# Beginning every second weight transfer of the experts' part on GpSimd instead of SyncE

## The chip, the cores and the metric

The kernel runs on one core of one Trainium2 chip. The metric is the device time of one launch in microseconds (us). TensorE (PE), VectorE (DVE), ScalarE (ACT), GpSimd (POOL) and SyncE (SP) each have an instruction stream of their own; 16 DMA engines move data between the chip's memory (DRAM here) and the on-chip buffers. Any engine's stream can begin a transfer; the transfer then runs by itself and tells of its landing through a semaphore.

## The reference

One decoder block over 256 tokens of width 1024: a modulated norm, one large input projection, a convolution branch and a gated recurrence branch that are merged and added to x, and then a mixture of 32 experts in which each token uses its top 4. Only the experts' part is touched by the change:

```python
logits = hf @ w_router + b_router
top_val, top_idx = lax.top_k(logits, 4)
top_w = softmax(top_val)
# for every token and each of its four experts e:
u = xb @ w1[e] + b1[e]                  # w1[e] is 1024 x 2048, float32
y = clamped_swiglu(u) @ w2[e] + b2[e]   # w2[e] is 1024 x 1024, float32
out[token] += top_w * y
```

All 32 experts are computed, so all of w1 and w2 is read: 32 times 12 MiB.

## The kernel before

The kernel has a first part (modulation, projection, the two branches, merge, router) and then the experts' part. All weights pass through one pool of 22 buffers (`NSLOT`) of 8 KB per partition. `queue` (L117) writes down what is to be loaded, in the order of use; `load` (L120) takes the next entry, takes a buffer and begins the transfer on SyncE (L123); `pump` (L126) decides how many loads are made whenever `free` returns a buffer. In the first part `pump` follows a plan, `LOADS`, whose entries add up to 88 loads. 73 entries stand in the queue ahead of the experts' weights, so the plan also makes the first 15 of the experts' loads. From L1207 on `spare` is a number: every freed buffer is used for the next load at once.

An expert takes 12 transfers of 1 MiB: 8 of w1 (`first_layer`, L972 to L999, matmuls on L987) and 4 of w2 (`second_layer`, matmuls on L1026). The last expert's w2 comes in 5 pieces with shorter rows, and one transfer of 512 KB (`gfin`) stands before the last expert.

Expert 0 to 31 follow one another in a Python loop, fully unrolled. From expert 3 on the loop is `inline`: after the first layer a branch (`tc.If`, L1247) looks whether the expert has more than 64 tokens and then treats a further 32 of them, and a second branch (L1278) does the second layer for these. The buffers of w1 are given back, all eight at once, only behind the first branch, those of w2 behind the second. Every engine executes these branches, each in its own stream.

After expert 21 (`RELOAD_AFTER`) stands `reload` (L1123), for tokens that fit nowhere else. It takes three buffers of the pool (`ring`, L1140), and its body, a loop over experts that loads weights with transfers begun on GpSimd, stands inside a branch at L1143. On the data here the body is not executed; each engine jumps over it. Behind the jump GpSimd's stream has a few semaphore instructions and one that brings the semaphores of its transfers to the counts which they would have if the body had run. The three buffers are given back right after (`free(3)`), and the next three loads of weights use them. x2, the residual stream, keeps one of the 22 buffers through the whole of the part.

In the experts' part the order of instructions is written out by hand for TensorE and SyncE (`manual_schedule`); GpSimd is not in that list, and it has no transfers and no arithmetic there. On SyncE a load waits for two things: for its buffer to be free, and for one of eight semaphores, which the loads take in turn, to be free again: the load eight places earlier must have landed.

Of the kernel before, what the change touches and what calls it, by code (L numbers as in the profile page):

```python
# [90 lines left out]
def block_kernel(ctx, tc, xT_d, x_d, prm_d, con_d, wada0_d, wada_d, bada_d, gfin_d, win_d, wco_d, who_d, wo_d,  # L91
                 wr_d, br_d, w1_d, b12_d, w2_d, out_d):
    nc = tc.nc
# [10 lines left out]
    loaded = {}  # L104
    plan = iter(LOADS)
    spare = None

    def slot(shape, name, dt=F32):
        live[0] += 1
        assert live[0] <= NSLOT, name  # L110
        return big.tile(shape, dt, tag="s", name=name)
# [8 lines left out]
    def load():  # L120
        key, shape, src, into = pending.pop(0)
        t = into if into is not None else slot(shape, "w_" + "_".join(map(str, key)), src.dtype)
        nc.sync.dma_start(out=t, in_=src)  # L123
        loaded[key] = t

    def pump():  # L126

        if spare is None:
            for _ in range(next(plan, 0)):
                load()  # L130
        else:
            while pending and live[0] < NSLOT - spare:
                load()

    def fetch(key):
        while key not in loaded:
            load()
        return loaded.pop(key)
# [1068 lines left out]
    spare = 0  # L1207
# [4 lines left out]
    for e in range(E_RUN):  # L1212
        i = e % 2
        hot = hot_of(e)
        spare = 3 if e == RELOAD_AFTER else 0
# [66 lines left out]
        if e == RELOAD_AFTER:  # L1282
            reload()
            spare = 0
# [132 lines left out]
```

## Time and profile before

| | us |
|---|---|
| median of 3 runs | 1334.53 |
| lowest and highest | 1331.17, 1335.19 |
| the profiled execution, as a run | 1334.8 |
| its span, first to last instruction | 1333.1 |
| busy: TensorE matmul | 1225.6 (92%) |
| busy: VectorE, ScalarE, GpSimd | 547.8, 274.2, 145.4 |
| bytes moved | 480.57 MB |

The span is the time from the first to the last instruction of one profiled execution; 1.7 us of that run lie around it. A busy TensorE is not a TensorE at its peak, and shares over the whole span mix the first part, in which GpSimd does arithmetic and the DMA engines have pauses, with the experts' part, in which GpSimd is idle and the DMA engines are not. The profile is therefore read by stretches.

### The profile page before, as it was taken

The numbers are of one execution on the slowest core, as the hardware profiler recorded it, in microseconds if no ns is written. First come the engines' busy times: TensorE is split into PE (matmuls) and PEld (weight loads), VectorE is DVE, ScalarE is ACT, GpSimd is POOL, SyncE is SP. The second block draws the span as 40 slices with busy tenths as digits, with TensorE's granted clock in tenths as the row PEclk, the third lists the DMA queues.
The fourth block names the chain that finished last, engine by engine and source line by source line (L and its number), as shares of the span: only waits on it lengthen the run. The fifth ranks groups of instructions, "written<-read, shape, count | busy, mean of one in ns | idle before, by whom it ended". The sixth has DMA issues, their size and how long they took to land. (4 is left out here: it accounts for less than half of the span.)

```text
span 1333.1 us, 18930 instructions
## 1 busy us (share of the span) xinstructions
PE 1225.6 (92%) x7761; PEld 671.4 (50%) x7761; DVE 547.8 (41%) x1065; ACT 274.2 (21%) x434; POOL 145.4 (11%) x63
## 2 busy tenths in 40 slices
PE   5999999999899999999899898888898889999997
PEld 3899877679864343443434333232333324334432
DVE  4498999645844242333223313222223312323322
ACT  4445534653321010101001000000000000000112
POOL 3257535122300000000000000000000000000000
PEclk8999989999999999999999999999899998999999
DMA  9993435646689999999999999999999999989994
GB/s 380 412 394 112 145 128 221 235 174 235 251 314 405 420 420 419 420 420 420 421 419 420 420 420 420 420 421 420 420 420 418 419 421 420 418 347 420 419 419 168
DMA packets 71493, 480.57 MB, mean 360 GB/s; under 512 B 7488, under 2 KB 8768, under 8 KB 16064
## 3 DMA queue, kind: packets, MB, share of 16 engines
q1 hardware_dynamic: 70928, 477.99, 88.0%
q8 instruction: 94, 1.54, 0.5%
q10 hardware_dynamic: 432, 0.72, 0.2%
q14 instruction: 39, 0.32, 0.1%
HBM read 477.63 MB, written 1.05 MB: 359 GB/s over the span
## 5 line engine op out<-in xcount | busy, mean ns | idle before, releaser
L987 PE MATMUL u_gl<-w_w,xg 128*64 128x512 f32 x1024 | 273.5, 599 | 23.5 <-DMA w_w<-in_w_dram 23.4
L987 PE MATMUL u_lin<-w_w,xg 128*64 128x512 f32 x1024 | 272.1, 594 | 0.8 <-issue 0.8
L1026 PE MATMUL yp<-w_w,li 128*64 128x512 f32 x992 | 223.3, 602 | 13.5 <-ACT li L1013 10.2
L994 DVE TENSOR_SCALAR gl<-u_gl 128x512 f32<-128x512 f32 (+1 forms) x33 | 22.3, 675 | 338.9 <-PE u_gl L987 338.9
L987 PEld LDWEIGHTS u_gl<-w_w,xg 128*64 128x64 f32 x1024 | 77.1, 137 | 166.7 <-issue 92.0
L987 PEld LDWEIGHTS u_lin<-w_w,xg 128*64 128x64 f32 x1024 | 81.9, 137 | 139.5 <-issue 139.5
L386 PEld LDWEIGHTS p_ps<-h,ws 128*128 128x128 f32 x1152 | 141.2, 193 | 11.7 <-issue 5.9
L386 PE MATMUL p_ps<-h,ws 128*128 128x256 f32 x1152 | 146.2, 287 | 0.0
L1026 PEld LDWEIGHTS yp<-w_w,li 128*64 128x64 f32 x992 | 69.1, 138 | 149.8 <-issue 128.0
L1036 DVE TENSOR_TENSOR yg<-yp,ga 64x512 f32<-64x512 f32 x60 | 41.3, 689 | 233.0 <-PE yp L1026 232.4
L372 POOL TENSOR_TENSOR ws<-w_in,ws 128x1024 fp32r<-128x1024 f32 x45 | 114.0, 2549 | 121.9 <-ACT ws L370 113.6
L995 ACT ACTIVATE u_gl<-gl 128x512 f32<-128x512 f32 (+1 forms) x33 | 19.4, 589 | 407.8 <-DVE gl L994 407.7
L437 DVE SCALAR_TENSOR_TENSOR cv<-u,pre,cv 128x255 f32<-128x255 f32 (+25 forms) x240 | 95.1, 456 | 9.1 <-ACT cv L434 8.3
L951 PE MATMUL xg_ps<-o,w_x 128*128 128x128 f32 (+1 forms) x544 | 68.6, 286 | 17.4 <-DVE li L996 10.3
L951 PEld LDWEIGHTS xg_ps<-o,w_x 128*128 128x128 f32 x544 | 65.0, 199 | 30.6 <-DVE li L996 21.7
L370 ACT CAST ws<-w_in 128x1024 fp32r<-128x1024 f32 x64 | 65.9, 1046 | 47.9 <-PE p_ps L386 25.0
L1039 ACT ACTIVATE ys0h<-yg,by 64x512 fp32r<-64x512 f32 x30 | 21.6, 720 | 244.0 <-DVE yg L1036 244.0
L955 DVE TENSOR_SCALAR xg<-xg_ps,g,sh 128x128 f32<-128x128 f32 (+1 forms) x136 | 45.4, 395 | 25.0 <-issue 16.6
L1013 ACT COPY li<-ta 128x512 f32<-128x512 f32 (+1 forms) x33 | 18.9, 573 | 120.6 <-PE ta L1010 120.6
L372 DVE TENSOR_TENSOR ws<-w_in,ws 128x1024 fp32r<-128x1024 f32 x19 | 25.0, 1331 | 14.0 <-ACT ws L370 14.0
L386 PE MATMUL wo_ps<-ws,mg 128*128 128x256 f32 x192 | 26.2, 297 | 3.5 <-ACT ws L370 1.8
L1040 DVE SCALAR_TENSOR_TENSOR ys0l<-yg,by,ys0h 64x512 fp32r<-64x512 f32 x30 | 22.4, 748 | 12.8 <-ACT ys0h L1039 11.9
(286 smaller groups left out, 1111.3 us busy)
## 6 DMA issues: line engine op xcount, KB each, us to landing
w_w<-in_w_dram SPq DMA_DIRECT2D x383, 1024.0 KB, 19.9
w_in<-in_win_dram SPq DMA_DIRECT2D x32, 1024.0 KB, 12.2
w_ada<-in_wada_dram SPq DMA_DIRECT2D x24, 1024.0 KB, 16.1
w_ho<-in_who_dram SPq DMA_DIRECT2D x4, 1024.0 KB, 4.7
w_co<-in_wco_dram SPq DMA_DIRECT2D x4, 1024.0 KB, 5.1
w_wo<-in_wo_dram SPq DMA_DIRECT2D x4, 1024.0 KB, 8.3
xT<-in_xT_dram SPq DMA_DIRECT2D x1, 1024.0 KB, 7.2
w_x<-in_x_dram SPq DMA_DIRECT2D x1, 1024.0 KB, 6.5
```

The source lines that it names most:

```text
L370: nc.scalar.copy(out=to[:, 0], in_=w[:, ks, :])
L372: (nc.vector if dve else nc.gpsimd).tensor_tensor(out=to[:, 1], in0=w[:, ks, :], in1=to[:, 0].bitcast(F32), op=ALU.subtract)
L386: nc.tensor.matmul(out, lhsT=lt, rhs=rh, start=first and kt == 0 and i == 0, stop=kt == KT - 1 and i == 2, skip_group_check=not first)
L437: nc.vector.scalar_tensor_tensor(out=cv[:, ct, s:], in0=u[i][:, m, :T - s], scalar=tap, in1=cv[:, ct, s:], op0=ALU.mult, op1=ALU.add)
L951: nc.tensor.matmul(ps[:, i, cs], lhsT=x2[:, t, kt * P:(kt + 1) * P], rhs=o[:, 0, t, cs], start=t == 0, stop=t == NT - 1)
L955: nc.vector.tensor_scalar(out=xg[h][:, i, cs], in0=ps[:, i, cs], scalar1=g2[:, kt:kt + 1], scalar2=sh2[:, kt:kt + 1], op0=ALU.mult, op1=AL ...
L987: nc.tensor.matmul(up[nb][g * 64:(g + 1) * 64, :], lhsT=xg[kt // 4][:, kt % 4, i * CAP:(i + 1) * CAP], rhs=w[:, c:c + 512], start=False, s ...
L994: nc.vector.tensor_scalar(out=gl[:, c], in0=up[0][:, c], scalar1=LIMIT, scalar2=None, op0=ALU.min)
L1026: nc.tensor.matmul(yp[g * 64:(g + 1) * 64, :], lhsT=aT[:, kt % 4, kt // 4, :], rhs=w[:, kk, g * 512:(g + 1) * 512], start=False, stop=kt = ...
L1036: nc.vector.tensor_tensor(out=y[rows, :], in0=yp[gs, :], in1=ga2[gs, :], op=ALU.mult)
L1039: nc.scalar.activation(hi[rows, :], y[rows, :], AF.Copy, scale=by[rows, :])
L1040: nc.vector.scalar_tensor_tensor(out=lo[rows, :], in0=y[rows, :], scalar=by[rows, :], in1=hi[rows, :].bitcast(F32), op0=ALU.mult, op1=ALU. ...
```

## The change

When `spare` is a number, that is for all loads that `pump` or `fetch` make from L1207 on, the list of the two issuers is turned round before each load, and the load is begun by its first entry. The first such load is begun by GpSimd, the next by SyncE, and so on. Shapes, buffers and the order of the list of loads stay.

```diff
@@ -104,6 +104,7 @@
     loaded = {}
     plan = iter(LOADS)
     spare = None
+    issuers = [nc.sync, nc.gpsimd]
@@ -120,7 +121,10 @@
     def load():
         key, shape, src, into = pending.pop(0)
         t = into if into is not None else slot(shape, "w_" + "_".join(map(str, key)), src.dtype)
-        nc.sync.dma_start(out=t, in_=src)
+
+        if spare is not None:
+            issuers.reverse()
+        issuers[0].dma_start(out=t, in_=src)
         loaded[key] = t
```

## Rows read from the trace of the kernel before

**Rows 1.** The page, part 2: the span in 40 equal slices.

```profile
PE   5999999999899999999899898888898889999997
...
DMA  9993435646689999999999999999999999989994
GB/s 380 412 394 112 145 128 221 235 174 235 251 314 405 420 420 419 420 420 420 421 419 420 420 420 420 420 421 420 420 420 418 419 421 420 418 347 420 419 419 168
```

**Rows 2.** Windows: the experts' part in three stretches, and within it 404 to 738.

```profile
core 0: us, PE busy (x) PEld busy (x) DVE busy (x) ACT busy (x) POOL busy (x), PEclk, DMA share, GB/s
389.00:738.00 349.00, 333.46 (x1664) 142.87 (x1660) 105.04 (x221) 34.00 (x51) 0.00 (x0) 1.00 1.00 414
738.00:1092.00 354.00, 311.90 (x1488) 122.33 (x1486) 98.50 (x204) 30.94 (x47) 0.00 (x0) 0.99 1.01 420
1092.00:1333.00 241.00, 219.76 (x1072) 92.29 (x1070) 64.33 (x135) 28.57 (x53) 0.00 (x0) 0.96 0.91 375
...
404.00:738.00 334.00, 318.46 (x1595) 137.83 (x1594) 102.58 (x216) 32.82 (x51) 0.00 (x0) 0.99 1.01 418
```

**Rows 3.** Waits of TensorE on transfers (total us, times, longest): 389:738, then 738:1092 (two).

```profile
PEld u_gl L987 <- DMA w_w<-in_w_dram: 3.0, 10, 0.6
...
PEld u_gl L987 <- DMA w_w<-in_w_dram: 66.8, 53, 2.1
...
PE u_gl L987 <- DMA w_w<-in_w_dram: 23.4, 44, 1.2
```

**Rows 4.** Timeline of TensorE around its last wait for a transfer (start, us, what).

```profile
1085.90 1.08 PE L987 MATMUL u_gl<-w_w,xg 128*64 128x512 f32 x4 [0.55 <-DMA w_w<-in_w_dram]
1086.81 1.03 PE L987 MATMUL u_lin<-w_w,xg 128*64 128x512 f32 x4
1088.38 1.08 PE L987 MATMUL u_gl<-w_w,xg 128*64 128x512 f32 x4 [0.55 <-DMA w_w<-in_w_dram]
1089.29 1.03 PE L987 MATMUL u_lin<-w_w,xg 128*64 128x512 f32 x4
```

**Rows 5.** Waits of SyncE's stream: 738:1092 (three rows), then 1092:1333 (two).

```profile
SPq L123 <- DMA w_w<-in_w_dram: 292.4, 139, 2.8
SPq L1143 <- SPq L1143: 5.2, 1, 5.2
SPq L123 <- PEq L1278: 0.7, 3, 0.3
...
SPq L123 <- DMA w_w<-in_w_dram: 111.6, 58, 2.5
SPq L123 <- PEq L1247: 34.3, 5, 16.6
```

**Rows 6.** Transfers begun (KB each, median us to landing): 700:760, then 310:330.

```profile
w_w<-in_w_dram SPq DMA_DIRECT2D x24, 1024.0 KB, 20.1
...
w_w<-in_w_dram SPq DMA_DIRECT2D x4, 1024.0 KB, 4.8
```

**Rows 7.** All instructions of L1143: duration ns min/median/max, first and last start us.

```profile
L1143 POOLq EVENT_SEMAPHORE  x5: 17/43/43, 404.1 to 404.4; - x5
...
L1143 POOLq COMPARE_BRANCH  x1: 45/45/45, 398.8 to 398.8; - x1
L1143 POOLq INC_SWDGE_SEM  x1: 172/172/172, 404.5 to 404.5; - x1
L1143 PEldq COMPARE_BRANCH  x1: 1166/1166/1166, 1013.1 to 1013.1; - x1
...
L1143 SPq COMPARE_BRANCH  x1: 45/45/45, 1033.5 to 1033.5; - x1
L1143 SPq EVENT_SEMAPHORE  x1: 17/17/17, 1038.7 to 1038.7; - x1
```

**Rows 8.** SyncE's instructions of L123, 1030:1041 (two rows); over the whole span (last).

```profile
L123 SPq EVENT_SEMAPHORE  x6: 17/22/28, 1032.7 to 1040.1; - x6
L123 SPq DMA_DIRECT2D w_w<-in_w_dram x5: 327/328/333, 1030.2 to 1040.2; - x5
...
L123 SPq DMA_DIRECT2D w_w<-in_w_dram x385: 327/328/8964, 299.4 to 1302.6; - x193
```

**Rows 9.** GpSimd's costliest group (page, 5), and VectorE's longest and L901's, 738:1092.

```profile
L372 POOL TENSOR_TENSOR ws<-w_in,ws 128x1024 fp32r<-128x1024 f32 x45 | 114.0, 2549 | 121.9 <-ACT ws L370 113.6
...
L1040 DVE SCALAR_TENSOR_TENSOR ys0l<-yg,by,ys0h 64x512 fp32r<-64x512 f32 x12 | 9.0, 748 | 5.1 <-ACT ys0h L1039 4.7
...
L901 DVE TENSOR_SCALAR o<-con,pos,r 128x64 f32<-128x64 f32 x24 | 5.9, 311 | 1.3 <-DVEq L1278 1.3
```

**Rows 10.** The page, part 3: DMA queues, packets, MB, share of 16 engines.

```profile
q1 hardware_dynamic: 70928, 477.99, 88.0%
q8 instruction: 94, 1.54, 0.5%
```

## The prediction

> **What bounds the kernel now.** I read the slices first, because the change touches one part only. From slice 13 on the DMA engines move 418 to 421 GB/s and are busy nine tenths, except in slices 35 and 39 (347 and 168 GB/s) [rows 1]. So the experts' part runs at one steady rate of transfer, and the first question is whether TensorE or this rate sets the end. The windows and the waits answer it by stretches.
>
> From 389 to 738 us TensorE is busy 333.46 of 349 us [rows 2] and waits for weights 3.0 us in all [rows 3]: it lives on buffers that were filled before, and is the bound. From 738 to 1092 the rate is 420 GB/s with a DMA share of 1.01 [rows 2], and TensorE's two kinds of waits for weights come to 66.8 and 23.4 us (they overlap, so they are not added) [rows 3]: here the DMA engines are the bound. The last of these waits ends at 1088.38, for the eighth piece of expert 24's w1 [rows 4]. From 1092 on no wait of TensorE for a transfer is in the answer; instead SyncE waits 34.3 us for buffers that TensorE gives back behind the branch at L1247 [rows 5]: the buffers are full again, and TensorE is the bound. The end therefore stands a fixed stretch of TensorE work behind that eighth piece: whatever moves its landing moves the end by the same amount, and what happens to transfers after it costs nothing while the filled buffers last. That landing is set by the bytes moved since about 404 us, when the engines became full.
>
> **The change part by part.** *What it moves.* The plan's 88 loads cover the 73 entries ahead of the experts and 15 of the 386 others (385 w_w [rows 8] and `gfin`); 371 remain, so GpSimd begins 186 and SyncE 185. Counting from 15, odd pieces go to GpSimd: of each expert's pieces every second one.
>
> *SyncE's relief.* An issue takes 328 ns [rows 8]; 185 fewer of them free 61 us of SyncE's stream. Worth nothing: in the middle stretch SyncE waits 292.4 us of 354 for a landing [rows 5], it is not short of time.
>
> *More in flight.* A load takes 20.1 us from issue to landing [rows 6]; 1.0486 MB at 420 GB/s take 2.5 us, so 20.1 / 2.5 = 8 are under way, the eight semaphores that SyncE's loads take in turn. With two issuers there may be up to 16. Engines with a share of 1.01 do not gain by a longer queue: 0. What is late next is the same rate.
>
> *GpSimd's issues.* No row shows GpSimd beginning a load. From below, SyncE's 0.33 us [rows 8]; from above, GpSimd's longest kind of instruction, 2.55 us [rows 9]. A load of GpSimd is due every 2 x 2.5 = 5 us, so either end is hidden behind its own queue; I take 1 us, nearer SyncE's since nothing is computed. If this cover is gone (an issue over 5 us) the order of landing breaks; that is the second rival. Here the Trainium skill speaks against the change (SBUF — State Buffer, section "SBUF: two separate sides", its box on VectorE blocking DMA): while VectorE runs one of its two-port modes, GpSimd cannot write the descriptors of a transfer that it begins. No run here shows it. By that rule, if all of VectorE's 98.50 us in the stretch locked it out, GpSimd would still have 255 us for some 70 loads, and the sum stays.
>
> *GpSimd's branches.* GpSimd now stands in the loop with its loads; in the trace of before it had run past L1143 by 404.5 us [rows 7]. Its branches take 45 ns, nothing queues behind them.
>
> *The jump over `reload`, the one new wait.* Behind the jump GpSimd has five semaphore instructions and one that raises the counts of its transfers' semaphores, 172 ns [rows 7]. In the kernel before, GpSimd has no transfer and passes in half a microsecond. With loads of its own under way, the counts can be raised only when each has landed. So GpSimd stops there until its last load from before the jump is in; queued behind it are all its later loads. SyncE is held too: its next three loads go into the buffers that the skipped body would have filled from GpSimd, and already now they carry extra waits for that (6 semaphore instructions around 5 loads at 1030 to 1041; GpSimd had raised the counts 630 us earlier) [rows 7, 8]. By then 264 pieces of experts 0 to 21 are used and 18 more fit the buffers (22 less x2's and the ring's three), so about 16 to 18 are under way, some 40 us of transfer. They land at the old rate, and then both queues are empty. The restart costs the raise, 0.17, an issue, 0.33, and the difference between a landing from an empty queue, 4.8 us [rows 6], and one in a full queue, 2.5: 0.17 + 0.33 + 2.3 = 2.8 us without transfer. Before, SyncE spent 5.2 us at that jump [rows 5] with eight loads under way, so nothing was lost; this cover is what goes. The place lies before the last wait at 1088, in the stretch that the transfers bound, so 2.8 us reach the end.
>
> *Order of landing.* Two queues that share the engines evenly land their pieces in pairs instead of one by one. The pair of the eighth piece of expert 24 (number 295, GpSimd's) ends when both are in, at the old time; if GpSimd's queue lags by up to one piece, it ends up to 2.5 us later. Between 0 and 2.5 I take 1.4, on the late side of the middle, because GpSimd restarts after the raise with the longer issue.
>
> *Rate of transfer.* Bytes from 404 to 1088 are the same: 684 us at 418 to 420 GB/s [rows 2]. No row shows a transfer of GpSimd. The nearest are the instruction loads, a second queue on the same engines: 94 packets of 1.54 MB took 0.5% of 16 x 1333.1 us, 1.13 us for 16 KB, against 0.64 us at the weights' rate (88.0% for 477.99 MB) [rows 10]: two queues share an engine roughly in halves, and the slices holding them stay at 418 to 421. That bounds a change of the whole rate by about 0.5% either way, 684 x 0.005 = 3.4 us. I take 0.
>
> Sum: 2.8 + 1.4 = 4.2 us, on the profiled execution's 1334.8: 1339.0. That run stands 0.3 above the median, which is no difference. About 0.3%, or 4 us, is what a measurement of this kernel can tell from no change, so the forecast lies on the edge of it.
>
> **The rivals.** *Nothing visible.* GpSimd's last load lands a little before SyncE's, its restart is hidden behind SyncE's, or the semaphores are counted so that nothing drains: 1335. For it speaks that the bound is a rate which the change doesn't touch; against it the instructions at L1143.
>
> *GpSimd's loads fall behind.* If its queue gets less than half of the engines, SyncE's pieces pile up and TensorE waits for every second piece. The buffers stop this: with eight w1 buffers held, 13 or 14 pieces may be ahead, 7 of them SyncE's, so the eighth piece of expert 24 comes at most 7 x 2.5 = 17.5 us late. With the restart: up to 1355. It decides from about two pieces of lag on. The rows on sharing speak against it [rows 10].
>
> *GpSimd's transfers run slower.* Each per cent of the rate costs 6.8 us by the end of the middle stretch; at 1.5%, with the restart, 1334.8 + 10.3 + 4.2 = 1349. The point from which it decides is a middle stretch under about 417 GB/s. The Trainium skill (DMA: Bandwidth & Descriptors, section "Latency and other measured facts") says that with transfers begun by GpSimd two of the 16 engines are usually slower, without a size. No run here shows it.
>
> *Faster.* If two queues keep the engines fuller, 1% gives 1328. Against it: no slice is above 421, at a share of 1.01.
>
> *It doesn't do what it says.* GpSimd's order isn't written out by hand, so its loads could be placed late in the stream; the time would be that of the second rival.
>
> **How the numbers follow.** Forecast (the drain and a small lag, 1337.6 to 1341): 0.45, about half of it over the edge. Nothing visible: 0.16. Behind or misplaced: 0.14. Slower rate: 0.15. Faster: 0.10. Slower by over 0.3%: 0.23 of the forecast, and 0.14 + 0.15 less 0.02 for small sizes of the two slow rivals, 0.50; faster 0.10; within, the remaining 0.40. The range takes the lower half per cent of rate (3.4 under 1334.8, 1331) and most of the two slow rivals, up to 1353.
>
> **What would show it.** The slices from 13 to 33 should stay at 418 to 421; a step that lowers all of them is the rate. Behind the jump, at about 1050 to 1060 us, there should be one pause of 2 to 3 us in the transfers, and a wait of GpSimd's and SyncE's streams there that the trace of before lacks. TensorE's last wait for a transfer should end 3 to 5 us later than 1088.4, and the work behind it take as long as now. Longer waits for odd pieces alone would be the lag. The prediction is wrong if the middle stretch isn't bound by transfers any more, or if waits for transfers appear behind 1092.

## The result, and the profile after

The changed kernel takes 1340.54 us, the median of six runs (1339.98 to 1346.9), against 1334.86 for the kernel before beside it (six runs, 1331.17 to 1337.41). The ratio is 1.0054, its 95% interval 1.0029 to 1.0079: slower, by about 6 us. The forecast was 1339.0 us. The profiled execution took 1340.64 us; its span is also 1339.0, 5.9 more than the span before. Behind line 104 every line number is now up to 4 higher: the load is L127, the matmuls of w1 L991, the skipped body's branch L1147.

The page's slices of the changed kernel (40 equal parts of the span, part 2) are to be compared with [rows 1], and its queues and its costliest group of GpSimd (parts 3 and 5) with [rows 10] and [rows 9]. The last two lines are the transfers begun from 700 to 760 us, as in [rows 6]:

```profile
DMA  9993335745689999999999999999999899989994
GB/s 382 411 388 127 128 127 221 252 176 213 253 328 420 420 418 418 421 420 420 420 419 421 420 420 420 420 420 420 420 421 417 333 420 421 421 342 421 419 420 175
...
q1 hardware_dynamic: 43248, 283.47, 52.4%
q0 software_dynamic: 27040, 194.52, 35.1%
...
L127 POOL DMA_DIRECT2D w_w<-in_w_dram x186 | 98.8, 533 | 828.3 <-PEq L1251 330.0
...
w_w<-in_w_dram SPq DMA_DIRECT2D x12, 1024.0 KB, 39.7
w_w<-in_w_dram POOLq DMA_DIRECT2D x12, 1024.0 KB, 39.7
```

The loads are divided as the diff says: 186 instructions of GpSimd, 0.533 us each, and 194.52 MB through a queue that the kernel before did not use for weights. A load in the full stretch now takes 39.7 us from issue to landing instead of 20.1 [rows 6], because 16 are under way and not 8, at 2.49 us each. From slice 13 to 34 the slices are what they were, with one exception: slice 31, from 1037 to 1071 us, moved 333 GB/s where before it had 419. The windows (time, then busy time of TensorE, its weight loads, VectorE, ScalarE and GpSimd, the granted clock, the DMA share and GB/s) place it; first the changed kernel:

```profile
404.00:1040.00 636.00, 577.06 (x2841) 241.51 (x2841) 184.99 (x386) 58.36 (x89) 66.99 (x127) 0.99 1.01 420
...
1030.00:1040.00 10.00, 9.22 (x44) 3.94 (x42) 2.77 (x4) 1.19 (x2) 0.00 (x0) 1.00 1.01 420
1040.00:1050.00 10.00, 9.84 (x50) 3.60 (x48) 3.19 (x6) 1.44 (x2) 0.00 (x0) 1.00 0.70 291
1050.00:1060.00 10.00, 7.96 (x37) 2.49 (x32) 1.55 (x7) 0.00 (x0) 3.68 (x7) 1.00 0.64 253
1060.00:1070.00 10.00, 5.89 (x29) 3.15 (x30) 3.05 (x5) 0.60 (x1) 1.58 (x3) 0.83 1.01 422
```

and the same view of the kernel before:

```profile
404.00:1040.00 636.00, 583.88 (x2855) 242.00 (x2856) 185.14 (x386) 59.09 (x91) 0.00 (x0) 0.99 1.01 419
...
1040.00:1050.00 10.00, 9.84 (x48) 3.37 (x44) 4.75 (x12) 1.44 (x2) 0.00 (x0) 1.00 1.01 418
1050.00:1060.00 10.00, 7.76 (x33) 1.94 (x32) 1.06 (x2) 0.51 (x1) 0.00 (x0) 1.00 1.01 423
```

636 us at 420 GB/s against 419: two issuers neither gain nor lose rate. Then 20 us of transfer are disturbed, and behind them the rate is the old one. What happened there is read from the instructions of the skipped body's branch in the changed kernel (duration in ns, min/median/max, then first and last start), which are to be compared with [rows 7], and from the waits of GpSimd and of SyncE on landings (total us, times, longest):

```profile
L1147 POOLq EVENT_SEMAPHORE  x5: 17/43/43, 1021.2 to 1051.6; - x5
...
L1147 SPq COMPARE_BRANCH  x1: 45/45/45, 1009.7 to 1009.7; - x1
L1147 SPq EVENT_SEMAPHORE  x1: 17/17/17, 1015.0 to 1015.0; - x1
...
L1147 POOLq COMPARE_BRANCH  x1: 45/45/45, 1015.8 to 1015.8; - x1
...
L1147 POOLq INC_SWDGE_SEM  x1: 742/742/742, 1051.7 to 1051.7; - x1
```

```profile
POOL w_w L127 <- DMA w_w<-in_w_dram: 184.4, 34, 37.1
...
SPq L127 <- DMA w_w<-in_w_dram: 369.9, 70, 37.4
```

GpSimd jumps over the body at 1015.8 and then stands at its five semaphore instructions until 1051.6, when its last transfer from before the jump has landed. Only then does it raise the counts, from 1051.7 to 1052.4. SyncE, which had jumped at 1009.7, stands for 37.4 us as well, since its next load goes into one of the body's buffers; it begins that load at 1052.53. In between the queues run dry. In [rows 7] the same five instructions passed in half a microsecond at 404 us, and the raise took 0.172 us.

TensorE's timeline in the changed kernel (start, duration, what, and in brackets the idle time before it with what ended it) shows how much later the weights come; the last two lines are to be compared with [rows 4]:

```profile
1057.52 1.08 PE L991 MATMUL u_gl<-w_w,xg 128*64 128x512 f32 x4 [1.50 <-DMA w_w<-in_w_dram]
1058.43 1.03 PE L991 MATMUL u_lin<-w_w,xg 128*64 128x512 f32 x4
1063.32 1.98 PE L991 MATMUL u_gl<-w_w,xg 128*64 128x512 f32 x4 [3.86 <-DMA w_w<-in_w_dram]
...
1093.99 1.08 PE L991 MATMUL u_gl<-w_w,xg 128*64 128x512 f32 x4 [1.28 <-DMA w_w<-in_w_dram]
1094.90 1.03 PE L991 MATMUL u_lin<-w_w,xg 128*64 128x512 f32 x4
```

The last wait for a transfer ends at 1093.99 and not at 1088.38: 5.6 us of the 5.9 are already there. From that wait to the end the trace has 245.0 us, before 244.7.

The landings themselves, put in the order of use, show two losses (us; worked out from the issue and landing of each load in the two traces; a piece is one load of 1 MiB, numbered from 0 in the order of use):

```
piece (expert, number)    before     after   begun by   later by
273  (22, w2 2nd)        1032.69   1035.23   GpSimd      +2.5
274  (22, w2 3rd)        1035.17   1033.78   SyncE       -1.4
281  (23, w1 6th)        1052.63   1051.40   GpSimd      -1.2
282  (23, w1 7th)        1055.12   1057.48   SyncE       +2.4
283  (23, w1 8th)        1057.60   1063.27   GpSimd      +5.7
284  (23, w2 1st)        1060.08   1063.08   SyncE       +3.0
294  (24, w1 7th)        1085.85   1088.37   SyncE       +2.5
295  (24, w1 8th)        1088.34   1093.95   GpSimd      +5.6
296  (24, w2 1st)        1090.82   1093.33   SyncE       +2.5
```

One loss is the restart: from the last old landing to the first new one there are 6.08 us (0.29 to the raise, 0.74 for it, 0.10 to SyncE's issue, 4.95 from that issue to the landing) where a full queue needs 2.49, so 3.6 are lost.

The other is the order, and it is older than the jump. Each of GpSimd's pieces lands together with the next one of SyncE, and SyncE's a little ahead of it: 274 before 273, as later 296 before 295. GpSimd's piece, which TensorE needs first, so comes about a whole piece later than from one queue (the **lag**). This is so in every pair from piece 71 to 277 (526 to 1045 us), with nothing held up at a jump yet: GpSimd's pieces land 2.0 to 3.5 us later than before, the last four of them 2.4 to 2.5, and SyncE's 0.7 to 2.3 earlier. In 295 the two add up: about 2.5 that were there before, and 3.1 that came at the jump.

### The profile page after: what moved, and what is told of

The parts are those of the page before. It is cut to its first block, busy times and chain, and to the rows that moved or that the text cites. A ratio compares the mean times of both kernels' runs of the same rounds, so it can differ in the third digit from the quotient of the medians.

```text
span 1339.0 us, 19142 instructions
## 1 busy us (share of the span) xinstructions
PE 1221.6 (91%) x7761; PEld 671.6 (50%) x7761; DVE 549.0 (41%) x1065; ACT 274.2 (20%) x434; POOL 244.3 (18%) x249
## 3 DMA queue, kind: packets, MB, share of 16 engines
q0 software_dynamic: 27040, 194.52, 35.1%
## 5 line engine op out<-in xcount | busy, mean ns | idle before, releaser
L991 PE MATMUL u_gl<-w_w,xg 128*64 128x512 f32 x1024 | 273.7, 599 | 31.6 <-DMA w_w<-in_w_dram 31.6
L991 PE MATMUL u_lin<-w_w,xg 128*64 128x512 f32 x1024 | 273.0, 596 | 1.0 <-issue 1.0
L127 POOL DMA_DIRECT2D w_w<-in_w_dram x186 | 98.8, 533 | 828.3 <-PEq L1251 330.0
L991 PEld LDWEIGHTS u_gl<-w_w,xg 128*64 128x64 f32 x1024 | 79.4, 137 | 168.9 <-issue 106.6
L991 PEld LDWEIGHTS u_lin<-w_w,xg 128*64 128x64 f32 x1024 | 82.4, 138 | 139.9 <-issue 139.9
L1043 ACT ACTIVATE ys0h<-yg,by 64x512 fp32r<-64x512 f32 x30 | 21.6, 719 | 244.7 <-DVE yg L1040 244.7
```

Of the source, the lines that this page charges most:

```text
L127: issuers[0].dma_start(out=t, in_=src)
L991: nc.tensor.matmul(up[nb][g * 64:(g + 1) * 64, :], lhsT=xg[kt // 4][:, kt % 4, i * CAP:(i + 1) * CAP], rhs=w[:, c:c + 512], start=False, s ...
L1043: nc.scalar.activation(hi[rows, :], y[rows, :], AF.Copy, scale=by[rows, :])
```

## Experiments

The theory (**drain**), as it stood before the runs: the time is lost at the jump alone, because a queue with transfers of its own must be empty there. Rivals: the alternation itself costs time everywhere; GpSimd's transfers are slower; GpSimd's queue falls behind. Each kernel was timed beside the kernel before, whose medians were 1334.7, 1335.1 and 1336.01 in the three groups of runs.

**1 and 2. No jump at all**, in the changed kernel (`alt_no_jump`) and in the kernel before (`sp_no_jump`). The body, which is not executed on this data, and its branch are left out.

```diff
-            skip_ahead(f"second{e}" if e != RELOAD_AFTER else "reload")
+            skip_ahead(f"second{e}")
@@
-            reload()
```

> The changed kernel without the branch at L1143 and its body (not executed on this data). Theory, the drain at the jump: nothing is left that waits for GpSimd's own transfers, the engines stay busy through 1040 to 1060 us, and the whole loss goes: within 1.5 us of the kernel before. Rival, transfers begun by GpSimd are dearer by themselves (issue, order of landing): the loss stays, 4 to 6 us over the kernel before.

> The kernel before without the same branch and body, the control for the run above. Theory: the jump cost the kernel before nothing, since eight loads were under way while SyncE stood at it: within 1 us of the kernel before. If the jump itself, with its 5.2 us, was on the path: about 2 to 5 us faster, and then the run above says less.

Measured: 1342.44 (ratio 1.0064, 1.0039 to 1.0089) and 1342.28 (1.006, 1.0036 to 1.0084). The surprise is the control: without the jump the kernel before is itself 7.6 us slower. For the transfers the theory holds. The windows of `alt_no_jump` have no gap:

```profile
1040.00:1050.00 10.00, 9.84 (x50) 3.50 (x48) 2.14 (x4) 1.44 (x2) 1.06 (x2) 1.00 1.01 420
1050.00:1060.00 10.00, 7.58 (x36) 2.19 (x33) 2.59 (x9) 0.00 (x0) 0.53 (x1) 1.00 1.02 424
```

and the bytes from 110 to 365 MiB took 636.6 us in both, as in the kernel before; in the changed kernel 643.8. The time was lost elsewhere. TensorE has a few stalls in this kernel for which the profile shows no wait ("issue"). In the kernel before the last of them stands in expert 24's w2, at 1098.8; in `sp_no_jump` it stands at 1262.6, where TensorE is the bound:

```profile
1257.11 2.05 PE L951 MATMUL xg_ps<-o,w_x 128*128 128x128 f32 x16 [0.78 <-DVE li L996]
1262.61 3.79 PE L951 MATMUL xg_ps<-o,w_x 128*128 128x128 f32 x16 [3.45 <-issue]
```

The kernel before does these 32 matmuls in 3.84 us without a break. From expert 26 to the end `sp_no_jump` needs 178.1 us, before 169.2. So a kernel without the jump differs in more than the jump, and the equal times of this pair (0.2 us apart) are not the price of the alternation: in `alt_no_jump` that stall is missing and the last wait of expert 24 ends 6.7 us later than in its control, about 3.3 of them from the first part. The other 3.4 are the order of landing, without any jump: piece 273 lands 6.8 us later than in the control, piece 274 only 3.3.

**3 and 4. A second jump**, behind expert 15, in the kernel before (`sp_two_jumps`) and the changed one (`alt_two_jumps`): this doubles the suspected cost and keeps the first place.

```diff
+JUMPS = (15, 21)
-        spare = 3 if e == RELOAD_AFTER else 0
+        spare = 3 if e in JUMPS else 0
-        if e == RELOAD_AFTER:
-            reload()
+        if e in JUMPS:
+            reload(e)
```

> The kernel before with a second jump of the same kind behind expert 15 (its body isn't executed either). The control for alt_two_jumps. Theory: no drain with SyncE alone, no pause of the transfers at either jump; the time moves only by TensorE's stalls without a wait, up to some 7 us either way.

> The changed kernel with the second jump behind expert 15. Theory, a drain costs about 7 us of transfers wherever the transfers are the bound: there are two pauses, the transfers fall back twice, and the kernel stands 12 to 14 us behind sp_two_jumps. Rival, the first jump's loss is made up by the longer queue before the second, or only one drain counts: 5 to 8 us.

Measured: 1334.51 (0.9998, 0.998 to 1.0015) and 1348.15 (1.0092, 1.0063 to 1.0121). A jump of itself costs the kernel before nothing that can be seen; with the alternation two of them cost 13.6 us over the control, where one cost 5.7. The slices of `alt_two_jumps`, and the raises among the instructions of its branches:

```profile
GB/s 384 410 382 125 141 115 219 262 181 195 271 328 417 422 417 418 421 419 421 419 420 420 421 420 418 328 415 420 420 420 416 357 420 421 421 341 420 420 419 174
```

```profile
L1148 POOLq INC_SWDGE_SEM  x2: 743/1446/2150, 871.7 to 1058.7; - x2
```

Two pauses (328 and 357 GB/s) where the control has 416 and 420, and one raise of 2.15 us. In the traces the last wait of expert 24 comes 9.0 us later than in the control, although the first part here was about 3 us shorter; the other 4.5 us of the spans lie behind it and were not followed up.

**5. SyncE alone around the jump** (`alt_quiet`): SyncE begins every load that is made while experts 19 to 21 run, so that GpSimd has nothing under way when it jumps.

```diff
+        quiet[0] = RELOAD_AFTER - 2 <= e <= RELOAD_AFTER
@@
+        (nc.sync if quiet[0] else issuers[0]).dma_start(out=t, in_=src)
@@
             reload()
+            quiet[0] = False
```

> The changed kernel with SyncE beginning all loads while experts 19 to 21 run, so that GpSimd has nothing under way when it reaches the jump behind 21; before and after that the two take turns as in the change. Theory: GpSimd passes the jump at once and the loss goes: within 1.5 us of the kernel before. Rival, the jump with the alternation around it costs by itself: 3 us or more stay.

Measured: 1347.33 (1.0093, 1.0063 to 1.0122), by its median slower than the change itself. The drain is gone: GpSimd raises its counts at 972.5, in 0.41 us, and the rate holds. But the pieces that TensorE needs come half as often (timeline, then windows of `alt_quiet`):

```profile
1048.08 1.97 PE L992 MATMUL u_gl<-w_w,xg 128*64 128x512 f32 x4 [2.24 <-DMA w_w<-in_w_dram]
1049.83 1.88 PE L992 MATMUL u_lin<-w_w,xg 128*64 128x512 f32 x4
1053.05 1.08 PE L992 MATMUL u_gl<-w_w,xg 128*64 128x512 f32 x4 [1.34 <-DMA w_w<-in_w_dram]
1053.95 1.03 PE L992 MATMUL u_lin<-w_w,xg 128*64 128x512 f32 x4
1058.02 1.69 PE L992 MATMUL u_gl<-w_w,xg 128*64 128x512 f32 x4 [3.03 <-DMA w_w<-in_w_dram]
```

```profile
1050.00:1060.00 10.00, 5.63 (x20) 1.25 (x18) 1.66 (x8) 0.00 (x0) 0.00 (x0) 0.84 1.01 420
1060.00:1070.00 10.00, 5.38 (x19) 1.06 (x16) 0.00 (x0) 0.00 (x0) 0.00 (x0) 0.84 1.02 423
```

The engines move 420 GB/s, but not what is needed next. At the jump SyncE's queue holds the next pieces of expert 23 and GpSimd's is empty; GpSimd begins pieces that are needed later (piece 285 lands at 1045.5, piece 276 at 1048.0), and from then on the two queues land one piece each by turns. SyncE's pieces land 4.97 us apart, twice 2.485. This is the rival "GpSimd's loads fall behind" with the engines' names changed: the engines are shared evenly by queue and not by need. The Trainium skill (DMA: Bandwidth & Descriptors, section "SWDGE vs HWDGE vs iDMA") says that the two kinds of issuers feed different queues inside each DMA engine, which serves them in turn; this trace agrees, with 4.97 against 2.485 us.

**6. SyncE alone until the bound has passed** (`alt_quiet_long`): the same from expert 19 to expert 26, so that the alternation starts again only where the buffers are full.

```diff
+        quiet[0] = RELOAD_AFTER - 2 <= e <= RELOAD_AFTER + 5
```

> As alt_quiet, but SyncE goes on beginning all loads until expert 26 is through, when the buffers are full and TensorE is the bound. Theory: with the drain gone and GpSimd's first new load no longer sharing the engines with pieces that are needed at once, both losses go, TensorE's last wait ends near 1088 us and the time is within 2 us of the kernel before. If the alternation between 404 and 975 us, with its larger number of transfers under way, costs by itself: 3 us or more stay.

Measured: 1334.29 (0.9995, 0.9978 to 1.0012). The last wait ends at 1088.56 (before 1088.38) and there is no slow slice between 12 and 34. Here GpSimd still begins every second load up to about 930 us and again behind expert 26, and that costs nothing. So the alternation costs nothing far from TensorE's last wait for a transfer. But the run takes away both losses at once, the drain and the order of landing at that wait, and can't tell one from the other.

**7 and 8. The jump moved behind expert 27**, where TensorE is the bound (`alt_jump27`, `sp_jump27`).

```diff
-RELOAD_AFTER = 21
+RELOAD_AFTER = 27
```

> The changed kernel with the jump behind expert 27 instead of 21. There TensorE is the bound and the buffers are full. Theory: the drain still takes place, and the transfers still pause for 4 to 8 us, but the filled buffers cover it: within 1.5 us of the kernel before. Rival, a drain delays the end wherever it stands: 4 to 6 us over the kernel before.

> The control for alt_jump27: SyncE alone, the jump behind expert 27. Theory: the place of the jump shifts what code TensorE runs where, and so the few microseconds that it loses without waiting for anything; the drain in alt_jump27 is covered. Then this kernel is as slow as alt_jump27, within 2 us. Rival, the drain costs there too: this kernel is at the level of the kernel before, 4 us or more below alt_jump27.

Measured: 1339.79 (1.0039, 1.0024 to 1.0054) and 1338.88 (1.0038, 1.0019 to 1.0056). The first alone speaks against the theory; its control takes that back. `alt_jump27` does drain, and harder (the branch, then the window):

```profile
L1147 POOLq INC_SWDGE_SEM  x1: 1462/1462/1462, 1236.8 to 1236.8; - x1
```

```profile
1230.00:1240.00 10.00, 9.24 (x44) 3.97 (x42) 2.76 (x4) 1.19 (x2) 0.53 (x1) 1.00 0.47 179
```

but no wait of TensorE for a transfer lies behind it, and the two kernels are 0.9 us apart. The 4 us that both lose come with the jump's new place, not with the drain: behind it both have, for one, two stalls of 1.51 and 1.19 us that end on VectorE, and from expert 26 to the end the two traces need 2.4 and 2.8 us more than the kernel before. (Both profiled runs, at 1336.81 and 1335.04, are faster than their medians: the stall in expert 24's w2 is missing in them.) The pair also shows the order of landing alone. The last wait of expert 24 with the alternation and without it:

```profile
1091.89 1.08 PE L991 MATMUL u_gl<-w_w,xg 128*64 128x512 f32 x4 [1.32 <-DMA w_w<-in_w_dram]
```

```profile
1089.34 1.08 PE L987 MATMUL u_gl<-w_w,xg 128*64 128x512 f32 x4 [0.55 <-DMA w_w<-in_w_dram]
```

It comes 2.6 us later, with no drain ahead of it. Of that 0.9 us, within the scatter of either, is left in the medians.

**9. The other queue** (`sp_body_sp`): in the kernel before, the skipped body's two transfers are written for SyncE instead of GpSimd. They are not executed here; only the queue that the branch has to bring to its counts is another.

```diff
-                                nc.gpsimd.dma_start(out=w, in_=w1_d[...
+                                nc.sync.dma_start(out=w, in_=w1_d[...
```

> The kernel before, SyncE alone, with one edit: the skipped body's transfers are written for SyncE instead of GpSimd. Theory: the drain belongs to the queue that the skipped body uses, not to GpSimd. SyncE then stops at the jump until its own eight loads have landed, the transfers pause, and the time is 4 to 7 us over the kernel before, although GpSimd begins nothing. Rival, only GpSimd's semaphores have to be raised by the engine itself: within 1 us of the kernel before.

Measured: 1337.83 (ratio 1.0001, 0.9984 to 1.0019). The mechanism is there without any load of GpSimd (the branch's instructions and the slices of `sp_body_sp`):

```profile
L1143 SPq EVENT_SEMAPHORE  x9: 17/17/17, 1041.5 to 1055.5; - x9
```

```profile
GB/s 383 410 390 121 135 128 221 233 146 264 245 294 409 421 421 418 420 420 420 421 420 421 420 420 420 420 422 420 420 420 418 334 422 420 421 413 421 420 419 170
```

SyncE stands from 1041.5 to 1055.5, slice 31 falls to 334 GB/s, the bytes take 643.3 us, and the last wait of expert 24 ends at 1094.2, 5.9 later than before. Its pieces were 2.7 to 2.9 late ahead of the jump already, so the restart alone is worth 3.0 to 3.2. But the expected 4 to 7 us of time are missing. Behind that wait TensorE's stall in expert 24's w2 is a different one here (`sp_body_sp`, then the kernel before):

```profile
1104.48 4.51 PE L1026 MATMUL yp<-w_w,li 128*64 128x512 f32 x20 [1.59 <-issue]
```

```profile
1098.80 9.14 PE L1026 MATMUL yp<-w_w,li 128*64 128x512 f32 x27 [3.19 <-issue]
```

From the eighth piece of expert 24 to expert 25 it takes 15.3 us instead of 20.1, and that gives back 4.8 us; 2.6 of them are lost again in expert 25, where TensorE here waits for transfers until 1124. The drain follows the queue of the skipped body; its price in the time of a run is not to be read from this kernel.

**10. All loads of the experts' part by GpSimd** (`all_gpsimd`): one queue, nothing to interleave.

```diff
-        if spare is not None:
-            issuers.reverse()
-        issuers[0].dma_start(out=t, in_=src)
+        issuers[spare is not None].dma_start(out=t, in_=src)
```

> All loads of the part begun by GpSimd alone, from the same line on. Theory: a transfer that GpSimd begins is no slower, so the engines stay at 418 to 421 GB/s between 404 and 1000 us with eight loads under way; the drain at the jump stays, with eight loads instead of sixteen to land: 4 to 7 us over the kernel before, like the changed kernel. If GpSimd's transfers or issues are dearer, the rate before the jump falls under 417 GB/s and the time rises by over 10 us.

Measured: 1340.12 (1.0037, 1.0021 to 1.0052). The window of `all_gpsimd` before the jump:

```profile
404.00:1040.00 636.00, 584.09 (x2856) 244.86 (x2858) 186.33 (x387) 58.83 (x90) 134.07 (x254) 0.99 1.01 420
```

420 GB/s: loads of GpSimd are as fast as SyncE's in a full queue. The drain is there as well, with a raise of 1.28 us and 313 GB/s in slice 31. With one queue there is no pair, so this kernel shows the drain without the change in order: the pieces are 0.7 to 1.0 us late just ahead of the jump and 6.1 behind it. The rival "slower transfers" is out.

## Why the prediction came out as it did

The time, 1340.54, lies 1.5 us above the forecast of 1339.0 and inside the range; slower by over 0.3% was the likeliest of the three. By its steps:

- *The bound.* It was right that the transfers bind from 738 to 1092 us and TensorE behind that, and in this pair the end does stand a fixed stretch behind the eighth piece of expert 24: 245.0 us, before 244.7. That is in part luck. Both traces have a stall of TensorE in expert 24's w2 (3.72 us, before 3.19) that the prediction did not count on, and it gives the later pieces time to land. In the seven traces in which that stall is shorter or missing, `sp_body_sp` among them, TensorE waits for transfers again in expert 25.
- *SyncE's relief, more in flight, the rate.* Worth nothing, as computed: 420 against 419 GB/s with twice as many loads under way, and the same in `all_gpsimd`. Two slower engines of the 16, as the Trainium skill has it (DMA: Bandwidth & Descriptors, section "Latency and other measured facts"), do not show in the rate of either kernel.
- *GpSimd's issue.* 0.533 us where 1 was taken between 0.33 and 2.55; hidden. None of the 127 issues from 404 to 1040 us took longer than 0.537, though VectorE was busy 185 us of the stretch, so VectorE's lock-out of GpSimd's descriptors (the Trainium skill, SBUF — State Buffer, section "SBUF: two separate sides") does not show in them.
- *The jump.* This was the one new wait, at the place named: GpSimd stands until its last load is in, SyncE with it. "1050 to 1060 us, one pause of 2 to 3 us" was an empty stretch from 1051 to 1053 in a disturbance from 1043 to 1055. The restart was sized at 2.8 and measures 3.6: the raise takes 0.74 and not 0.17 (that figure came from a queue without transfers, the only row there was), and the semaphore instructions around it take 0.4; against that, the issue of 0.33 was counted twice, since the 4.8 us to a landing run from the start of the issue. The raise took from 0.17 to 2.15 us in these traces, so one row of it said little.
- *The order of landing.* 1.4 was taken between 0 and 2.5; it measures about 2.5, a whole piece, the upper end. The sum paired 295 with 294 and let it end "at the old time"; in the trace it lands with 296, and so at the old time of 296. The reason given for the size, that GpSimd restarts later, fails: the same lag is there before the jump, and without any drain ahead in `alt_jump27` and `alt_no_jump`.
- *The sum.* Piece 295 is 5.6 late: 2.5 of order and 3.1 of the jump, instead of 1.4 and 2.8. The restart's 3.6 become 3.1 because the last old piece, 281, had landed 1.2 early, while the first pair behind the restart took 5.8 us instead of 5.0; some of the 1.2 comes from the first part, the rest is open. So both terms were too small, the order by 1.1 us and the jump by 0.3; behind the wait the longer stall adds 0.5.
- *The rivals.* "Falls behind" did not happen in the change, but it is real: `alt_quiet` brings it about with an uneven start and loses 12.6 us by it. "Nothing visible" is what `alt_quiet_long` shows once no load of GpSimd crosses the jump or is needed at TensorE's last wait.

What the bytes show is more than what TensorE lost: from 110 to 365 MiB the changed kernel needs 7.2 us more, while SyncE's pieces are 2.5 late. From 1043 to 1051 us the DMA share was only 0.57. Probably some of the 16 engines had finished their parts of the last loads while the others still worked, so that the bytes fell behind without any piece landing later; the trace does not tell the engines apart, and this was not tested.

So the theory of the experiments was half right: the time is not lost at the jump alone. Drain and lag are shown by their landings in the traces. In the time of a run the drain shows in the pair of 3 and 4 (13.6 us for two jumps) and in `all_gpsimd` (4.1 us); the lag by itself does not: the pairs 1 and 2, 7 and 8 leave 0.2 and 0.9 us. How the 5.7 us divide rests on single traces, whose first parts differ by up to 3 us. That GpSimd's pieces lag because they are the first of each pair is worked out from the landings; beginning with SyncE instead was not tried. A version that keeps the alternation and has no drain (`alt_quiet_long`) equals the kernel before; none was faster.

## What to carry to other kernels

A conditional body that is skipped still has to account for the transfers written in it: in these kernels the queue which it would use had to be empty at the jump, on GpSimd and on SyncE alike. So keep that queue free of other transfers, or put the jump where filled buffers hide a restart. Where the engines are full, a second issuer gives no rate, and it splits them by queue and not by need: with turns taken piece by piece, the first of each pair landed a piece late, and pieces that are needed next should not stand in the longer of two queues. A control with the same edit in the kernel before belongs beside every such experiment; here two of the four kernels that changed only the jump of the kernel before lost 4 and 7.6 us of their own.

## What was not expected of the hardware

TensorE's stall without a wait has two forms, and the clock tells them apart. Windows of the kernel before around the stall of 3.19 us at 1095.6 (the granted clock is the third number from the right):

```profile
1090.00:1095.00 5.00, 4.31 (x20) 2.42 (x19) 2.27 (x4) 1.19 (x2) 0.00 (x0) 1.00 1.01 421
1095.00:1099.00 4.00, 0.81 (x5) 0.20 (x4) 0.00 (x0) 0.00 (x0) 0.00 (x0) 0.86 1.02 418
1099.00:1104.00 5.00, 5.00 (x14) 1.27 (x14) 0.00 (x0) 0.00 (x0) 0.00 (x0) 0.50 1.01 421
1104.00:1108.00 4.00, 3.95 (x17) 1.04 (x13) 0.02 (x1) 0.00 (x0) 0.00 (x0) 0.91 1.02 424
```

and of `sp_body_sp` around its stall of 1.59 us:

```profile
1100.00:1104.00 4.00, 2.79 (x12) 0.78 (x12) 0.00 (x0) 0.04 (x1) 0.00 (x0) 1.00 1.01 414
1104.00:1108.00 4.00, 3.52 (x18) 1.24 (x20) 0.00 (x0) 0.00 (x0) 0.00 (x0) 1.00 1.02 424
```

After 3.19 idle microseconds TensorE runs five at 0.50 of its clock (1.2 of 2.4 GHz), 27 matmuls in 9.14 us; after 1.59 idle ones it stays at 1.00 and does 20 in 4.51. At full clock the 27 would take 6.1 (27 times 4.51/20), so the longer stall costs some 3 us more than its own length. A load of 16 KB of instructions, from 1096.4 to 1097.4, lies inside the longer one. Leaving out or moving a part of the program moves these stalls (1262.6 in `sp_no_jump`), and in that trace the stretch from expert 26 to the end is 8.9 us longer. In the trace of `sp_jump27` the same stretch is 2.8 us longer, nearly all of it the two stalls that end on VectorE; the 4 us by which its median is longer are not shown in full. What gives a stall its place and its length was not tried.
